# Layer C's prompt attention with key tiles of 128, 128 and 16, and a new order of the steps of layers C and D

## The chip, the core and the metric

The kernel runs on one core of a Trainium2 chip, as one launch. The metric is the device time of that launch in microseconds. A core has five engines that work side by side, each through its own instructions in order: TensorE (PE, matrix products; PEld is its loading of the stationary operand), VectorE (DVE), ScalarE (ACT), GpSimd (POOL) and SyncE (SP, which here only issues DMAs). Engines wait for each other by semaphores.

## The reference, cut to what matters

Four layers of different kinds act on 336 tokens: 64 of a running stream (the "sample") and 272 of a new one (16 meta tokens and 256 frames, the "prompt"). Layers A and B are two recurrences; the change leaves them alone. Layer C is attention over a compressed cache, layer D a convolution of 31 taps along time for each of 2048 channels.

```python
def mla_mixer(...):                                   # layer C, 16 heads
    q_lat, kv_lat, k_pe, g = split(u @ w_in)          # g: gate path
    s = (q_abs . keys_c + q_pe . keys_pe) * C_SCALE
    mask = k_chunk[None, :] <= q_chunk[:, None]       # chunks of 64 frames, meta tokens first
    p = softmax(where(mask, s, -inf))
    o = p @ values
    return (o * silu(g)) @ w_out

def conformer_mixer(...):                             # layer D
    a, b, g = split(u @ w_in)
    v = a * sigmoid(b)
    c = causal_dwconv(concat(buf, v), conv_w) + conv_b   # 31 taps
    c = silu(layernorm(c))
    return (c * silu(g)) @ w_out
```

A prompt frame sees the meta tokens, its own chunk of 64 and the chunks before. The 16 meta queries see only the 16 meta keys, so the queries of the prompt's rows 16 to 79 see 80 keys, the next 144, then 208, and the last 272. The sample's 64 queries see 528 cached keys and their own 64.

## The kernel before

Everything lies transposed: features on the 128 partitions, the 336 tokens along the free dimension. A weight tile is 128x1024 float32. It comes from memory on SP's queue (`wraw`, three buffers), ACT casts it to a rounded part (`whi`, line 323) and the difference (`wlo`, line 335) is taken on DVE, or on POOL for the tiles named in the list `PRM["lo"]`. PE then makes three products for each slice (`mm3`: high by high, high by low, low by high). The tile of weights for one gate or input column (`in_tile`) is 24 matmuls of 336 columns. `Weights.tick` and `step` run the casts some tiles ahead. In the other layers' products of plain float32 the trace shows two matmul passes for each call.

**Layer C** first makes its latent queries and keys (the head: `raw_tile` six times, `rope`, `kv`, `qn`, `tk`, where `tk` transposes the sample's new keys), and then works through eight pairs of heads. Each pair p has steps: `q0`, `q1` (queries, PE), `sqa`, `ssc`, `str`, `sol`, `sou` (sample: absorb, scores and softmax, transposes, latent output, output), and for each head t of the pair `psc`, `pso`, `ptr`, `pou` (prompt: scores, softmax, transposes, output); `k` and `v` make keys and values for two pairs at a time; `g` is a gate tile, 24 matmuls that depend on no step. `PRM["c"]` lists the steps with a lag each, and `c_steps` unrolls it; this is the order of the instructions on every engine. PSUM banks are few: `acc` has two, and `misc`, `sp`, `pt`, `o`, `ss` one each, so a step that writes `misc` waits until the reader of the step before is done. The prompt's scores of a head lie in one tile `P` of 128 rows by 432 columns, queries 16 to 143 with 144 keys, queries 144 to 271 with 272 keys, and the meta queries with 16. In `p_tr` PE transposes it in six pieces, three of 128 keys into `pt`, three of 16 meta keys into `misc` (one of them 16x16); ACT copies the first, DVE the second. `p_out` multiplies them by the values, with key tiles 0 to 15, 16 to 143 and 144 to 271: three products of 272, 256 and 128 columns, the first with only 16 rows.

**Layer D** makes input tiles b and a for each of 16 column tiles j, `dext` from them on DVE, stores it to memory and loads it back shifted (`store`, `shifts`, on SP's queue) so that `conv_pe` can do four taps in one group of four 32-column products. `npm[j]` is the number of such groups, `ngt[j]` the taps that ACT scales and POOL adds (`gq`, `gp`), and DVE does the rest (`conv_dve`, line 1621, a generator run by `pump`). `conv_pe(j)` comes two column tiles after j. Gate tiles lie between (`PRM["g"]`, `tg`). After column tile 15 the sums over all channels (`s`, made on POOL) go through PE for the mean and the variance; nothing of layer D's output can start ahead of that, but for gate tiles 14 and 15.

## Time and profile before

| | us |
|---|---|
| median of three runs (lowest and highest) | 1310.57 (1309.44 to 1312.44) |
| the profiled execution | 1316.76 |
| its span, from the first to the last instruction | 1315.0 |
| busy in it: PE, DVE, ACT, POOL | 1259.6, 893.1, 776.4, 290.4 |

All rows below come from that one profiled execution. Times in them count from its first instruction. Layer C runs from about 640 to 993, layer D from about 998 to the end. A matmul's end is modelled, and matmuls overlap; so what one costs in a stream is read from start to start and not from its duration.

### The profile page before, as it was taken

The numbers are of one execution on the slowest core, as the hardware profiler recorded it, in microseconds if no ns is written. First come the engines' busy times: TensorE is split into PE (matmuls) and PEld (weight loads), VectorE is DVE, ScalarE is ACT, GpSimd is POOL, SyncE is SP. The second block draws the span as 40 slices with busy tenths as digits, with TensorE's granted clock in tenths as the row PEclk, the third lists the DMA queues.
The fourth block names the chain that finished last, engine by engine and source line by source line (L and its number), as shares of the span: only waits on it lengthen the run. The fifth ranks groups of instructions, "written<-read, shape, count | busy, mean of one in ns | idle before, by whom it ended". The sixth has DMA issues, their size and how long they took to land.

```text
span 1315.0 us, 21810 instructions
## 1 busy us (share of the span) xinstructions
PE 1259.6 (96%) x8402; PEld 1185.7 (90%) x8402; DVE 893.1 (68%) x1654; ACT 776.4 (59%) x1448; POOL 290.4 (22%) x335
## 2 busy tenths in 40 slices
PE   8999999999999999899989999998999899999896
PEld 8999999999999999799879898887898789888795
DVE  5677666676658999957755555555657498886684
ACT  5677666667545877755554445444643756665563
POOL 0000000000001122100140000000002676878592
PEclk9999999999999999899989999899999899999999
DMA  6433343333441444344343222231242576767242
GB/s 211 142 124 92 125 126 107 131 126 104 137 145 66 145 145 145 113 147 144 110 158 105 88 89 81 67 99 60 91 150 71 165 199 179 208 178 196 77 139 74
DMA packets 58903, 166.25 MB, mean 126 GB/s; under 512 B 7616, under 2 KB 22048, under 8 KB 58800
## 3 DMA queue, kind: packets, MB, share of 16 engines
q1 hardware_dynamic: 55248, 157.28, 38.6%
q0 software_dynamic: 1504, 4.88, 1.2%
q10 hardware_dynamic: 2048, 2.70, 0.7%
q8 instruction: 66, 1.08, 0.3%
q14 instruction: 37, 0.30, 0.1%
HBM read 157.34 MB, written 7.50 MB: 125 GB/s over the span
## 4 chain that ended last, share of the span: by engine, by line
PE 71%; DVE 12%; ACT 6%; issue 3%; POOL 3%; DMA 2%; SPq 0%; ACTq 0%; DVEq 0%; POOLq 0%
PE acc L395 41%; PE bacc L395 9%; PE cv L395 3%; PE o L395 3%; PE hacc L395 3%; DVE wlo L335 2%; PE y L395 2%; PE sp L395 2%; ACT Pp L1450 2%; PE ss L395 2%; ACT whi L323 1%; PE misc L395 1%; DVE cv L1621 1%; POOL wlo L335 1%; DMA wraw<-in_wts_dram 1%
## 5 line engine op out<-in xcount | busy, mean ns | idle before, releaser
L395 PE MATMUL acc<-uh,whi 128*128 128x336 f32 x1208 | 390.5, 323 | 1.8 <-ACT vv L979 1.8
L395 PE MATMUL acc<-uh,wlo 128*128 128x336 f32 x1208 | 384.2, 318 | 0.0
L395 PE MATMUL acc<-ul,whi 128*128 128x336 f32 x1208 | 383.5, 317 | 0.0
L323 ACT ACTIVATE whi<-wraw 128x1024 fp32r<-128x1024 f32 (+2 forms) x263 | 269.0, 1028 | 91.2 <-DMA wraw<-in_wts_dram 64.0
L335 DVE TENSOR_TENSOR wlo<-wraw,whi 128x1024 fp32r<-128x1024 f32 (+2 forms) x233 | 286.1, 1243 | 25.2 <-ACT whi L323 24.7
L395 PEld LDWEIGHTS acc<-uh,whi 128*128 128x128 f32 x1208 | 228.8, 189 | 11.6 <-issue 5.0
L395 PEld LDWEIGHTS acc<-ul,whi 128*128 128x128 f32 x1208 | 228.9, 189 | 0.5 <-issue 0.2
L395 PEld LDWEIGHTS acc<-uh,wlo 128*128 128x128 f32 x1208 | 227.9, 189 | 0.0
L687 POOL TENSOR_TENSOR x<-x,sroot 128x336 f32<-128x336 f32 x6 | 5.3, 897 | 533.5 <-ACT sroot L675 390.6
L1621 DVE SCALAR_TENSOR_TENSOR cv<-dext,dw,cv 128x366 f32<-128x366 f32 x184 | 97.3, 594 | 3.5 <-PE cv L395 2.7
L1613 POOL TENSOR_TENSOR gp<-gp,gq 128x366 f32<-128x366 f32 x77 | 90.0, 1170 | 36.1 <-ACT gq L1612 32.2
L395 PE MATMUL bacc<-oh,whi 128*128 128x336 f32 x288 | 92.1, 320 | 0.0
L395 PE MATMUL bacc<-oh,wlo 128*128 128x336 f32 x288 | 91.3, 317 | 0.0
L395 PE MATMUL bacc<-ol,whi 128*128 128x336 f32 x288 | 91.1, 316 | 0.0
L335 POOL TENSOR_TENSOR wlo<-wraw,whi 128x1024 fp32r<-128x1024 f32 (+1 forms) x30 | 67.3, 2248 | 18.2 <-ACT whi L323 18.2
L395 PE MATMUL acc<-oh,whi 128*128 128x336 f32 x192 | 61.5, 320 | 1.9 <-ACT dsg L1665 1.1
L395 PE MATMUL acc<-ol,whi 128*128 128x336 f32 x192 | 61.1, 318 | 1.3 <-DVE ol L421 0.8
L395 PE MATMUL acc<-oh,wlo 128*128 128x336 f32 x192 | 60.9, 317 | 0.7 <-DVE wlo L335 0.7
L1450 ACT ACTIVATE Pp<-sp,mx 64x80 f32<-64x80 f32 (+4 forms) x80 | 30.0, 375 | 45.9 <-DVE mx L1448 26.0
L395 PEld LDWEIGHTS bacc<-ol,whi 128*128 128x128 f32 x288 | 54.2, 188 | 0.4
L395 PEld LDWEIGHTS bacc<-oh,whi 128*128 128x128 f32 x288 | 54.2, 188 | 0.4
L395 PEld LDWEIGHTS bacc<-oh,wlo 128*128 128x128 f32 x288 | 54.1, 188 | 0.0
(436 smaller groups left out, 2561.8 us busy)
## 6 DMA issues: line engine op xcount, KB each, us to landing
wraw<-in_wts_dram SPq DMA_DIRECT2D x243, 512.0 KB, 3.6
dsh<-dxt SPq DMA_DIRECT2D x60, 189.0 KB, 4.2
wraw<-in_wts_dram SPq DMA_DIRECT2D x16, 384.0 KB, 3.0
dxt<-dext SPq DMA_DIRECT2D x15, 198.0 KB, 4.1
out_hg_dram<-sf SPq DMA_DIRECT2D x16, 128.0 KB, 2.1
wraw<-in_wts_dram SPq DMA_DIRECT2D x8, 256.0 KB, 2.7
ukt<-in_ukt_dram POOLq DMA_DIRECT2D x8, 256.0 KB, 3.3
uv<-in_wts_dram POOLq DMA_DIRECT2D x8, 256.0 KB, 3.9
```

What stands on the lines that cost most here:

```text
L323: self.nc.scalar.activation(hi[:, :n], self.raw[i][:, :n], AF.Copy)
L335: e.tensor_tensor(lo[:, :n], self.raw.pop(i)[:, :n], hi[:, :n].bitcast(F32), op=OP.subtract)
L395: self.PE.matmul(out, l, r, start=start, stop=stop)
L687: G.tensor_tensor(self.x[:, k], self.x[:, k], sq, op=OP.mult)
L1450: A.activation(P[r0:r1, c:c + n], s[r0:r1, c:c + n], AF.Exp, scale=C_SCALE, bias=mx[r0:r1, j:j + 1], accum_out=sm[r0:r1, j:j + 1])
L1613: G.tensor_tensor(cv[j, "p"], cv[j, "p"], q, op=OP.add)
L1621: V.scalar_tensor_tensor(c[:, :T], ext[j % NX][:, n:n + T], tap(n, j), c[:, :T], op0=OP.mult, op1=OP.add)
```

## The change

Layer C: the values are made for key tiles 0 to 127, 128 to 255 and 256 to 271. `P` is 544 columns wide, holds the long part first, and is zero where nothing is written. `p_tr` makes one product with 16 columns of the identity and five transposes of 128x128, and reads over the zeros, so that all pieces have 128 rows and 128 columns; `pl` (128x64, zero but for 16 rows) holds the last 16 keys. `p_out` then has products of 272, 192 and 64 columns, each with 128 rows. The third product of `values` has a stationary operand of 16 columns. In the head, the cache comes in five DMAs, where it was eight; the constant `k_pair` is gone, and two products by columns take its place; the sample's new keys stand behind the cached ones; their evacuation is on DVE.

The tables: `c` has one gate tile behind `tk`, one less in pair 1, and in pair 2 one ahead of the softmax of head 1 where it was behind its transposes. In D `npm[9]` is 3 (was 4), `ngt` and `pump` change, and the gate tiles near the end stand later. 15 tiles' `wlo` go from DVE to POOL (ten of layer C, five of D), four of D go back.

```diff
--- before.py
+++ after.py
@@ -35,27 +35,28 @@
...
-    "npm": [0, 2, 4, 3, 3, 2, 4, 3, 4, 4, 4, 4, 4, 4, 4, 3],
+    "npm": [0, 2, 4, 3, 3, 2, 4, 3, 4, 3, 4, 4, 4, 4, 4, 3],
...
-    "ngt": [5, 5, 2, 6, 4, 7, 4, 3, 7, 7, 9, 7, 3, 9, 1, 14],
-    "act": [1, 9, 6, 79, 2],
...
-    "g": [0, 0, 0, 0, 1, 0, 1, 0, 2, 1, 1, 0, 1, 0, 1, 0],
...
+    "ngt": [3, 5, 2, 6, 6, 7, 4, 3, 7, 8, 8, 7, 2, 10, 1, 15],
+    "act": [0, 8, 7, 80, 2],
...
+    "g": [0, 0, 0, 0, 1, 0, 1, 0, 2, 1, 1, 0, 1, 0, 0, 0],
...
-    "tg": [3, 2],
...
+    "tg": [2, 2],
...
+          ["do1", 15], ["do1", 13], ["do1", 6], ["da", 2], ["do1", 5], ["do1", 3], ["do1", 11], ["cg", 6], ["cg",
+          2], ["da", 13], ["db", 15], ["cg", 4], ["co2", 11], ["dg", 7], ["cun", 2], ["da", 4], ["dg", 12], ["co2",
+          15], ["cg", 7], ["cup", 6], ["cup", 4], ["co2", 8], ["da", 10]],
...
-        "k_pair": np.ascontiguousarray(pm.reshape(128, -1)),
...
+            G.memset(keyk[:48, 4], 0.0)
...
-            loads = [(keyt[:, l, a:b], self.d["ct"][:, l, c:d])
-                     for l in range(2) for a, b, c, d in ((0, 512, 0, 512), (576, NK, 512, NCACHE))]
-            loads += [(kps[:, :512], self.d["cr"][:, :512]), (kps[:, 576:], self.d["cr"][:, 512:]),
-                      (keyk[:, :4], self.d["ck"]), (keyk[64:80, 4], self.d["ckt"])]
+
+            loads = [(keyt[:, l, :NCACHE], self.d["ct"][:, l]) for l in range(2)]
+            loads += [(kps[:, :NCACHE], self.d["cr"]), (keyk[:, :4], self.d["ck"]), (keyk[48:64, 4], self.d["ckt"])]
...
-            G.tensor_copy(keyt[:, :, 512:576], kr[:, :, :NS])
-            G.tensor_copy(kps[:, 512:576], kpe[:, :NS])
+            G.tensor_copy(keyt[:, :, NCACHE:], kr[:, :, :NS])
+            G.tensor_copy(kps[:, NCACHE:], kpe[:, :NS])
...
-            A.activation(keyk[:64, 4], tp[:64, :256], AF.Copy)
+            V.tensor_copy(keyk[64:, 4], tp[:64, :256])
...
+            pl = [tm.tile([128, 64], F32, name=f"ppl{t}") for t in range(2)]
             for t in range(2):
-                z = tm.tile([128, 432], F32, name=f"Pp{t}")
+                G.memset(pl[t], 0.0)
+                z = tm.tile([128, 544], F32, name=f"Pp{t}")
...
-                        V.tensor_tensor(qs, qp[:, :NS].unsqueeze(1).to_broadcast([128, 2, 64]), pm, op=OP.mult)
+                        for h in range(2):
+                            V.tensor_scalar(qs[:, h], qp[:, :NS], self.col(f"m{h}"), None, op0=OP.mult)
...
-                for j, (c, w) in enumerate(((0, 16), (16, 128), (144, 128))):
-                    a = self.acc()
-                    z = slice(c, c + 128)
+                G.memset(vt[:, 2], 0.0)
+                for j, (c, w) in enumerate(((0, 128), (128, 128), (256, 16))):
+                    a = self.acc()[:w]
+                    z = slice(c, c + w)
                     for k in range(2):
                         self.mm3(a, kvh[:, k, z], kvl[:, k, z], h[:, k], l[:, k], k == 0, k == 1)
-                    A.activation(vt[:w, j], a[:w], AF.Copy)
+                    A.activation(vt[:w, j], a, AF.Copy)
...
-                self.PE.transpose(b[:80, :128], P[:, 512:], self.ident)
+                self.PE.transpose(b[:, :128], P[:, NK - 128:], self.ident)
                 pt = tm.tile([128, 5, 128], F32, name="spt")
                 A.activation(pt[:, :4].rearrange("p a b -> p (a b)"), a, AF.Copy)
-                V.tensor_copy(pt[:80, 4], b[:80, :128])
+                V.tensor_copy(pt[:, 4], b[:, :128])
...
+                         (0, 16, 416, 16, 2, 416))
+                for r0, r1, c, n, j, _ in parts:
                     V.tensor_reduce(mx[r0:r1, j:j + 1], s[r0:r1, c:c + n], axis=AX, op=OP.max)
                 V.tensor_scalar(mx, mx, -C_SCALE, None, op0=OP.mult)
-                for r0, r1, c, n, j in parts:
-                    A.activation(P[r0:r1, c:c + n], s[r0:r1, c:c + n], AF.Exp, scale=C_SCALE, bias=mx[r0:r1, j:j + 1],
+                for r0, r1, c, n, j, o in parts:
+                    A.activation(P[r0:r1, o:o + n], s[r0:r1, c:c + n], AF.Exp, scale=C_SCALE, bias=mx[r0:r1, j:j + 1],
                                  accum_out=sm[r0:r1, j:j + 1])
                 rs = tm.tile([128, 3], F32, name="rs")
                 V.reciprocal(rs, sm)
-                V.tensor_scalar(P[:, :144], P[:, :144], rs[:, 0:1], None, op0=OP.mult)
-                V.tensor_scalar(P[:, 144:416], P[:, 144:416], rs[:, 1:2], None, op0=OP.mult)
-                V.tensor_scalar(P[:16, 416:], P[:16, 416:], rs[:16, 2:3], None, op0=OP.mult)
+                V.tensor_scalar(P[:, :272], P[:, :272], rs[:, 1:2], None, op0=OP.mult)
+                V.tensor_scalar(P[:, 272:416], P[:, 272:416], rs[:, 0:1], None, op0=OP.mult)
+                V.tensor_scalar(P[:16, 416:432], P[:16, 416:432], rs[:16, 2:3], None, op0=OP.mult)
...
             def p_tr(p, t):
                 P = Pp[t][0]
...
-                tr(a[:, 0:128], P[:, 16:144], self.ident)
-                tr(a[:, 128:256], P[:, 160:288], self.ident)
-                tr(a[:, 256:384], P[:, 288:416], self.ident)
-                tr(b[:16, 0:16], P[:16, 416:432], self.ident[:16, :16])
-                tr(b[:16, 16:144], P[:, 0:16], self.ident)
-                tr(b[:16, 144:272], P[:, 144:160], self.ident)
-                pt = tm.tile([128, 384], F32, name="ppt")
-                pm_ = tm.tile([16, NP], F32, name="ppm")
-                A.activation(pt, a[:, :384], AF.Copy)
-                V.tensor_copy(pm_, b[:16, :NP])
-                H[p, t] = (pt, pm_)
+                self.mm(a[:, 0:16], P[:, 416:544], self.ident[:, :16])
+                tr(a[:, 208:336], P[:, 400:528], self.ident)
+                tr(a[:, 16:144], P[:, 272:400], self.ident)
+                tr(a[:, 144:272], P[:, 0:128], self.ident)
+                tr(a[:, 336:464], P[:, 128:256], self.ident)
+                tr(b[:, :128], P[:, 256:384], self.ident)
+                pt = tm.tile([128, 464], F32, name="ppt")
+                A.activation(pt, a[:, :464], AF.Copy)
+                V.tensor_copy(pl[t][:16], b[:16, 64:128])
+                H[p, t] = pt
 
             def p_out(p, t):
-                pt, pm_ = H.pop((p, t))
+                pt = H.pop((p, t))
                 vt = quadw[p // 2][1]
                 z = slice(128 * (2 * (p % 2) + t), 128 * (2 * (p % 2) + t) + 128)
                 o = bank("o")
-                self.mm(o[:, :NP], vt[:16, 0, z], pm_, True, False)
-                self.mm(o[:, 16:NP], vt[:, 1, z], pt[:, :256], False, False)
-                self.mm(o[:, 144:NP], vt[:, 2, z], pt[:, 256:], False, True)
+                self.mm(o[:, :NP], vt[:, 0, z], pt[:, :272], True, False)
+                self.mm(o[:, 80:NP], vt[:, 1, z], pt[:, 272:], False, False)
+                self.mm(o[:, 208:NP], vt[:, 2, z], pl[t], False, True)
```

On PE, a prompt head's transposes and output, at pair 1 of layer C. `Pp` is the tile P, `pt` and `misc` are PSUM, `ppt` and `ppm` or `ppl` are the copies, `vt` the values. Before:

```order
L1462 MATMUL pt<-ident,Pp_7262 128x128
L1463 MATMUL pt<-ident,Pp_7262 128x128
L1464 MATMUL pt<-ident,Pp_7262 128x128
L1465 MATMUL misc<-ident,Pp_7262 16x16
L1466 MATMUL misc<-ident,Pp_7262 16x128
L1467 MATMUL misc<-ident,Pp_7262 16x128
L395 MATMUL o<-ppm,vt 128x272
L395 MATMUL o<-ppt,vt 128x256
L395 MATMUL o<-ppt,vt 128x128
```

And in the changed kernel:

```order
L395 MATMUL pt<-ident,Pp_7261 128x16
L1468 MATMUL pt<-ident,Pp_7261 128x128
L1469 MATMUL pt<-ident,Pp_7261 128x128
L1470 MATMUL pt<-ident,Pp_7261 128x128
L1471 MATMUL pt<-ident,Pp_7261 128x128
L1472 MATMUL misc<-ident,Pp_7261 128x128
L395 MATMUL o<-ppt,vt 128x272
L395 MATMUL o<-ppt,vt 128x192
L395 MATMUL o<-ppl_7259,vt 128x64
```

The pieces of 16 rows and 16 columns are gone, and the products are 272, 192 and 64 columns wide, each from 128 rows.

On DVE, at pair 2 of layer C, from the queries' mask (`qs`) on; `mx` is the softmax's maximum of head 1, `sg<-sq,acc` a gate tile's evacuation. Before:

```order
L1328 TENSOR_TENSOR qs<-qp,pm 128x128
L1447 TENSOR_REDUCE mx_7270<-sp 64x1 x4
L1447 TENSOR_REDUCE mx_7270<-sp 16x1
L1448 TENSOR_SCALAR mx_7270<-mx_7270 128x3
L1453 RECIPROCAL rs<-sm_7271 128x3
L1454 TENSOR_SCALAR Pp_7268<-Pp_7268,rs 128x144
L1455 TENSOR_SCALAR Pp_7268<-Pp_7268,rs 128x272
L1456 TENSOR_SCALAR Pp_7268<-Pp_7268,rs 16x16
L1471 COPY ppm<-misc 16x272
L335 TENSOR_TENSOR wlo<-wraw,whi 128x1024
L1203 SCALAR_TENSOR_TENSOR sg<-sq,acc 128x336
```

And in the changed kernel:

```order
L1329 TENSOR_SCALAR qs<-qp,vec 128x64 x2
L335 TENSOR_TENSOR wlo<-wraw,whi 128x1024
L1201 SCALAR_TENSOR_TENSOR sg<-sq,acc 128x336
L1450 TENSOR_REDUCE mx_7270<-sp 64x1 x4
L1450 TENSOR_REDUCE mx_7270<-sp 16x1
L1451 TENSOR_SCALAR mx_7270<-mx_7270 128x3
L1456 RECIPROCAL rs<-sm_7271 128x3
L1457 TENSOR_SCALAR Pp_7268<-Pp_7268,rs 128x272
L1458 TENSOR_SCALAR Pp_7268<-Pp_7268,rs 128x144
L1459 TENSOR_SCALAR Pp_7268<-Pp_7268,rs 16x16
L1475 COPY ppl_7258<-misc 16x64
```

The evacuation of a gate tile, and the split of a weight tile ahead of it, now stand ahead of the softmax of head 1, which they followed.

On ACT, near the end of layer D's convolution, from the last tap that ACT scales for column tile 15 (`gq`); `dsg` is a gate's SiLU, `call` a convolution's finished column tile. Before (the cast of 128x768 is the first of the output weights):

```order
L1612 ACTIVATE gq<-dext_10632,dw 128x366 x2
L323 ACTIVATE whi<-wraw 128x768
L1665 ACTIVATE dsg<-acc 128x336
L1633 ACTIVATE call<-cv,vec 128x64
L1634 ACTIVATE call<-cv,vec 128x272
L1636 ACTIVATE sq<-call 128x336
```

And in the changed kernel:

```order
L1616 ACTIVATE gq<-dext_10628,dw 128x366
L323 ACTIVATE whi<-wraw 128x1024
L1669 ACTIVATE dsg<-acc 128x336
L1637 ACTIVATE call<-cv,vec 128x64
L1638 ACTIVATE call<-cv,vec 128x272
L1640 ACTIVATE sq<-call 128x336
```

The finished tiles now follow the SiLU of gate tile 11, where they followed that of tile 12. On PE one gate tile (24 matmuls) stood between the last `conv_pe` and the mean; now three stand there (72).

## Rows read from the trace of the kernel before

**Rows 1.** Page, part 1: busy time, share of the span, instructions.

```profile
PE 1259.6 (96%) x8402; PEld 1185.7 (90%) x8402; DVE 893.1 (68%) x1654; ACT 776.4 (59%) x1448; POOL 290.4 (22%) x335
```

**Rows 2.** Stretches: time, busy time and instructions by engine, granted clock, DMA share, GB/s.

```profile
645.00:653.00 8.00, 7.88 (x49) 7.41 (x49) 4.67 (x6) 4.97 (x12) 1.10 (x2) 1.00 1.00 325
841.00:848.00 7.00, 6.65 (x32) 6.09 (x32) 1.60 (x5) 0.87 (x2) 1.69 (x4) 0.56 0.47 151
1180.00:1200.00 20.00, 20.00 (x161) 16.64 (x151) 8.44 (x18) 10.28 (x20) 18.56 (x14) 1.00 0.71 192
```

**Rows 3.** Timeline, PE, an output of pair 0: start, duration, engine, line, operation [idle before <-releaser].

```profile
710.23 1.00 PE L395 MATMUL misc<-olat,uv 128*128 128x64 f32 x8
711.15 0.72 PE L395 MATMUL o<-ppm,vt 16*128 16x272 f32 x2
...
712.56 1.05 PE L395 MATMUL misc<-qn,ukt 128*128 128x64 f32 x8
713.42 0.40 PE L395 MATMUL acc<-uh,whi 128*128 128x336 f32 x1
```

**Rows 4.** Timeline, PE, pair 0, transposes of head 1.

```profile
720.91 0.27 PE L1462 MATMUL pt<-ident,Pp 128*128 128x128 f32 x1
...
721.13 0.27 PE L1464 MATMUL pt<-ident,Pp 128*128 128x128 f32 x1
721.34 0.18 PE L1465 MATMUL misc<-ident,Pp 16*16 16x16 f32 x1
...
721.59 0.38 PE L395 MATMUL ss<-ksh,qabh 128*128 128x296 f32 x1
721.81 0.30 PE L395 MATMUL ss<-ksl,qabh 128*128 128x296 f32 x1
```

**Rows 5.** Timeline, PE, pair 4, scores of head 1 and the sample's output.

```profile
831.10 0.41 PE L395 MATMUL sp<-kp,qp 128*128 128x144 f32 x2
831.35 0.62 PE L395 MATMUL sp<-kn,qn 128*128 128x272 f32 x2
831.81 0.62 PE L395 MATMUL sp<-kp,qp 128*128 128x272 f32 x2
...
839.27 0.77 PE L395 MATMUL misc<-olat,uv 128*128 128x64 f32 x5 [0.89 <-DVE ppm L1471]
```

**Rows 6.** Timeline, DVE and ACT, pair 4, softmax of head 1.

```profile
833.68 1.56 DVE L1447 TENSOR_REDUCE mx<-sp 64x1 f32<-64x80 f32 x5
...
837.96 0.18 DVE L1453 RECIPROCAL rs<-sm 128x3 f32<-128x3 f32 x1 [2.51 <-ACT Pp L1450]
...
838.79 0.42 DVE L1471 COPY ppm<-misc 16x272 f32<-16x272 f32 x1
...
839.15 0.42 ACT L1202 ACTIVATE sq<-acc 128x336 f32<-128x336 f32 x1
```

**Rows 7.** Timeline, ACT and DVE, head of layer C.

```profile
653.48 1.06 ACT L323 ACTIVATE whi<-wraw 128x1024 fp32r<-128x1024 f32 x1 [3.51 <-DMA wraw<-in_wts_dram]
...
659.28 1.22 DVE L335 TENSOR_TENSOR wlo<-wraw,whi 128x1024 fp32r<-128x1024 f32 x1
```

**Rows 8.** Timeline, PE and SP's queue, layer D.

```profile
1078.10 2.05 PE L395 MATMUL cv<-dsh,dcw 128*32 128x366 f32 x24 [1.38 <-DMA dsh<-dxt]
...
1060.40 5.77 SPq L304 DMA_DIRECT2D wraw<-in_wts_dram  x2
```

**Rows 9.** Timeline, DVE and PE, end of layer D's convolution.

```profile
1219.72 4.65 DVE L1621 SCALAR_TENSOR_TENSOR cv<-dext,dw,cv 128x366 f32<-128x366 f32 x9 [2.75 <-PE cv L395]
...
1226.63 2.33 PE L395 MATMUL cv<-s,onesE 128*128 128x336 f32 x4 [3.08 <-POOL s L1640]
1228.76 1.33 PE L395 MATMUL cv<-call,onesE 128*128 128x336 f32 x2
```

**Rows 10.** Timeline, POOL and DVE, two splits at once.

```profile
1203.17 2.40 POOL L335 TENSOR_TENSOR wlo<-wraw,whi 128x1024 fp32r<-128x1024 f32 x1
...
1204.60 2.06 DVE L335 TENSOR_TENSOR wlo<-wraw,whi 128x1024 fp32r<-128x1024 f32 x1
```

More of the change, by code (lines that the diff above doesn't have):

```diff
@@ L44 @@
     "bt": [3, 1, 9, 13, 15, 24, 18, 9, 12, 6, 16, 17, 18, 24],
-    "npm": [0, 2, 4, 3, 3, 2, 4, 3, 4, 4, 4, 4, 4, 4, 4, 3],
+    "npm": [0, 2, 4, 3, 3, 2, 4, 3, 4, 3, 4, 4, 4, 4, 4, 3],
     "idle": [12, 8],
-    "ngt": [5, 5, 2, 6, 4, 7, 4, 3, 7, 7, 9, 7, 3, 9, 1, 14],
-    "act": [1, 9, 6, 79, 2],
-    "pump": [[9, 8, 3, 0, 4], [6, 4, 6, 0, 6]],
[9 rows of a table removed]
+    "ngt": [3, 5, 2, 6, 6, 7, 4, 3, 7, 8, 8, 7, 2, 10, 1, 15],
+    "act": [0, 8, 7, 80, 2],
+    "pump": [[8, 6, 2, 0, 4], [4, 4, 6, 0, 5]],
[10 rows of a table added]
 }
@@ L1178, in layer_c @@
             rp = cp.tile([128, 2, NT], F32, name="rp")
-            pm = cp.tile([128, 2, 64], F32, name="pm")
             ksh = cp.tile([128, 3, NK], F32R, name="ksh")
@@ L1183, in layer_c @@
             keyk = cp.tile([128, 5, 256], F32, name="keyk")
+            G.memset(keyk[:48, 4], 0.0)
             kps = wt.tile([128, NK], F32, name="kps")
             nc.gpsimd.dma_start(rp.rearrange("p a b -> p (a b)"), self.d["k_rope"])
-            nc.gpsimd.dma_start(pm.rearrange("p a b -> p (a b)"), self.d["k_pair"])
-            loads = [(keyt[:, l, a:b], self.d["ct"][:, l, c:d])
-                     for l in range(2) for a, b, c, d in ((0, 512, 0, 512), (576, NK, 512, NCACHE))]
-            loads += [(kps[:, :512], self.d["cr"][:, :512]), (kps[:, 576:], self.d["cr"][:, 512:]),
-                      (keyk[:, :4], self.d["ck"]), (keyk[64:80, 4], self.d["ckt"])]
+            loads = [(keyt[:, l, :NCACHE], self.d["ct"][:, l]) for l in range(2)]
+            loads += [(kps[:, :NCACHE], self.d["cr"]), (keyk[:, :4], self.d["ck"]), (keyk[48:64, 4], self.d["ckt"])]
             def rope(out, ps):
@@ L1412, in s_olat @@
                     for j in range(5):
-                        w = 128 if j < 4 else 80
-                        self.mm(a[:, 128 * l:128 * l + 128], keyk[:w, j, 128 * l:128 * l + 128], pt[:w, j], j == 0, j == 4)
+                        self.mm(a[:, 128 * l:128 * l + 128], keyk[:, j, 128 * l:128 * l + 128], pt[:, j], j == 0, j == 4)
                 o = tm.tile([128, 2, 128], F32, name="olat")
@@ L1444, in p_soft @@
                 P, mx, sm = Pp[t]
-                parts = ((0, 64, 0, 80, 0), (64, 128, 0, 144, 0), (0, 64, 144, 208, 1), (64, 128, 144, 272, 1), (0, 16, 416, 16, 2))
-                for r0, r1, c, n, j in parts:
+                parts = ((0, 64, 0, 80, 0, 272), (64, 128, 0, 144, 0, 272), (0, 64, 144, 208, 1, 0), (64, 128, 144, 272, 1, 0),
+                         (0, 16, 416, 16, 2, 416))
+                for r0, r1, c, n, j, _ in parts:
                     V.tensor_reduce(mx[r0:r1, j:j + 1], s[r0:r1, c:c + n], axis=AX, op=OP.max)
                 V.tensor_scalar(mx, mx, -C_SCALE, None, op0=OP.mult)
-                for r0, r1, c, n, j in parts:
-                    A.activation(P[r0:r1, c:c + n], s[r0:r1, c:c + n], AF.Exp, scale=C_SCALE, bias=mx[r0:r1, j:j + 1],
+                for r0, r1, c, n, j, o in parts:
+                    A.activation(P[r0:r1, o:o + n], s[r0:r1, c:c + n], AF.Exp, scale=C_SCALE, bias=mx[r0:r1, j:j + 1],
                                  accum_out=sm[r0:r1, j:j + 1])
```

18 rows, old and new, of the table PRM are left out of this document.

## The prediction

> **What bounds the kernel now.** I read part 1 of the page first: PE is busy 1259.6 of 1315.0 us [rows 1], so only work on PE, or a wait of PE, can move the end. I then went through PE's timeline of layers C and D, subtracting a stream's usual spacing, and looked at what released each idle stretch. The reader is to see three things. First, layer C holds pieces that cost more than their columns: between two runs of eight 64-column passes, three products take 712.56 - 710.23 = 2.33 us, eight passes included [rows 3]. Second, the waits are short and end in DVE's queue, as the 0.89 us ahead of the sample's output in pair 4 [rows 5]. Third, layer D loses most at one place, the barrier at its end, where PE stands idle 3.08 us and then works slowly [rows 9].
>
> **Layer C, outputs.** The same eight passes with nothing foreign behind them take 713.42 - 712.56 = 0.86 us, so the three products with their changes of shape cost 2.33 - 0.86 = 1.47 us [rows 3]. After, they are two passes of each width. A pair of 272 columns takes 831.81 - 831.35 = 0.46, one of 144 columns 831.35 - 831.10 = 0.25 [rows 5], so 192 columns take about 0.33 by the line between. A 64-column pass takes 0.86 / 8, so the third pair 0.22. Together 1.00. The saving is 0.47 for each of 16 heads, **-7.5 us**. About 0.11 of the 0.47 is columns (528 instead of 656, at 0.46 / 272 for a pair's column, less the floor that the 64-column pair pays); the other 0.36 is the change between operands of 16 and of 128 rows, which goes. This is the largest term, and what it rests on is that the changes cost and not something that follows them.
>
> **Layer C, transposes.** Before, six pieces take 721.59 - 720.91 = 0.68, and the next product starts its successor 0.22 after itself where others do after 0.13 to 0.14 [rows 4]: 0.77 in all. After, there are seven passes (the product with the identity is two); the one that follows a transpose of the same shape comes 0.11 later (two steps from 720.91 to 721.13) [rows 4], so 0.77. **Nothing**, from -2.5 if passes of 16 columns take half that to +1 us.
>
> **Layer C, values.** The third product now has a stationary operand of 16 columns. The step into such a form is 721.34 - 721.13 = 0.21 where 0.11 is usual, so 0.10; the way out I take as 0.18, the larger of the two sides of the output's changes. Four times 0.28: **+1.1 us**.
>
> **Layer C, waits.** In pairs 4 and 6 the sample's output waits 0.89 us for the copy of the transposes [rows 5], which on DVE stands behind head 1's softmax. That chain does not shorten, but PE comes 0.47 earlier by the cheaper output ahead of it. The copy is 0.2 shorter (64 columns), and the queries' mask is two instructions where it was one, about 0.1 longer. So PE waits 0.37 more at both: **+0.7**. In pair 2 a gate tile now precedes the softmax on DVE, as the order shows. From its last matmul on there are its SiLU on ACT, 0.42 [rows 6], its product on DVE, which I estimate at 0.48 from the copy's 0.42 for 272 columns, and then maximum to copy, 838.79 + 0.42 - 833.68 = 5.5 less 0.2 [rows 6]: 6.2 us. PE has the transposes, an output and one gate tile in that time, 0.77 + 1.00 + 24 x 0.16 = 5.6, the 0.16 being 7.88 us / 49 matmuls [rows 2]. That leaves 0.6, and the steps from engine to engine add to it: **+0.7**, between 0 and +1.5. These stay small because each is paid once.
>
> **Layer C, head.** One split of 1.22 us on DVE, between two steps of the chain that PE waits for [rows 7], goes to POOL: -1.2. Against it, the cached keys' transposed copy is now loaded sooner, into a stretch in which the DMA engines are full (share 1.00, 325 GB/s, 645 to 653) and ACT waits 3.51 us for a weight tile [rows 2, 7]. Its 524 KB at 325 GB/s are 1.6 us; if the half of it lands ahead of the weights, +0.8. One evacuation less on ACT, -0.2. **-0.6**, from -3.5 to +1.5. Sum of layer C: -7.5 + 1.1 + 0.7 + 0.7 - 0.6 = **-5.6 us**.
>
> **Layer D, one tap group less.** `npm[9]` loses four products of two passes. A tile with three groups has 24 passes in 2.05 us [rows 8]; eight passes fewer are 0.68 by that, less something for a fixed part: **-0.6**. The taps that it takes over are on DVE (+3 in all, 4.65 / 9 = 0.52 each [rows 9]); DVE works 8.44 of 20 us in the stretch before the end [rows 2], so they hide there. If that cover is gone, 1.5 us.
>
> **Layer D, a late transfer.** At 1078.10 PE waits 1.38 us for a shifted tile [rows 8]. SP's queue, which issues it, stood 5.77 us at a weight tile whose buffer a split on POOL still held [rows 8]. That split (`da` 5) goes back to DVE, where one takes 1.22 [rows 7]. But `da` 4 goes to POOL just ahead. **-0.9**, between -1.4 and +1.
>
> **Layer D, the end.** Before, one gate tile lies between the last `conv_pe` and the mean, and PE waits 3.08 us for POOL's sums; its first four passes of 336 columns then take 1228.76 - 1226.63 = 2.13 us [rows 9], where 0.46 / 2 for 272 columns [rows 5] makes 4 x 0.28 = 1.1. After, three gate tiles lie there, 2 x 24 x 0.16 = 7.7 us more cover, while conv 15 comes no later than DVE's 2.75 us wait for it allows [rows 9]. I take the wait, 1.3 for the slow passes (1.0 in these four, 0.3 in those behind) and 0.4 for small gaps, an estimate: **-4.8**, from 0 to -5.2. What is late next: ACT's taps, 15 of the last tile instead of 14, and POOL's sums behind them; they have 4 us of margin. Sum of layer D: -0.6 - 0.9 - 4.8 = **-6.3 us**.
>
> **The sum.** -11.9 us. The profiled execution would go from 1316.76 to 1304.9; it is 6.2 above the median of 1310.57, and what lies outside the span stays at 1.8. By the median: 1310.57 - 11.9 = **1298.7 us**. A measurement of this kernel can tell 0.2%, 2.6 us.
>
> **Rivals.** (A) The changes of rows cost nothing of their own, and what follows them absorbs it. Then layer C's outputs save the columns alone, 16 x 0.11 = 1.8, and 5.7 of the sum goes: 1304.4 us. Against it stands that the pair of 272 columns with 128 rows takes 0.46 [rows 5], while the whole group of 656 columns, some 1.1 by that rate, took 1.47 [rows 3]. The Trainium skill, "TensorE: Matmul & The Clock Gate", section "Why this matters for your kernels", says that a single product with 32 rows takes the time of one with 128; by that rule zeros instead of few rows bring nothing. The trace differs, at the changes at least, by the 0.36 us above. Chance 0.06.
>
> (B) The end does not move: with POOL given five more splits in D, at 18.56 busy of 20 us just before [rows 2], its sums come as late relative to the gate tiles as before. Then -4.8 goes: 1303.5. Against it stands the 7.7 us of cover. Chance 0.10.
>
> (C) Slower. Seven splits of layer C now on POOL run beside DVE's chain from softmax to copy. Two splits side by side took 2.40 on POOL and 2.06 on DVE [rows 10] where DVE alone needs 1.22 [rows 7]. If each stops a DVE instruction of that chain for its whole 2.4 us, and PE's waits there are already above zero [rows 5], 7 x 2.4 = 16.8 us come on top: 1315.5. It decides as soon as a split starts just ahead of a rotation or a difference with two operands in the chain, and the chain has no slack. Against it: 2.06 - 1.22 = 0.84 is what one overlap cost, and most splits have a gate tile's 24 x 0.16 = 3.8 us ahead of them. The Trainium skill, "SBUF — State Buffer", section "Who interferes with whom", says that a DVE instruction with two SBUF inputs contends with a GpSimd instruction that reads SBUF; the trace agrees, by these 0.84 us. Chance 0.08.
>
> (D) The new short waits bring a fall of the clock. From 841 to 848 the granted clock is 0.56 with PE busy 6.65 of 7 us [rows 2], behind the wait at 839.27 [rows 5]: 7 x 0.44 = 3.1 us. Three more of them: +9.2, 1307.9. Chance 0.06.
>
> **How the numbers follow.** The forecast has 0.70, the rest is shared as said: A .06, B .10, C .08, D .06. Range: the open ends are the head (-2.9, +2.1), the transposes (-2.5, +1), the late transfer (-0.5, +1.9) and the end (-0.4, +4.8). Not all fall together: 1291 below; above, 1308, which takes in A, B and D and leaves out C and the sum of several bad ends. Faster by more than 0.2% means below 1307.9: forecast, A, B and most of D, 0.86. Same: the rest of D and of the forecast's own tail, 0.06. Slower: C, 0.08.
>
> **What would show it.** In the changed profile: the three outputs from start to next product in 1.0 us; transposes and the next start in 0.77; PE's wait for sums at the end gone, with the granted clock near 1 there; the wait at the sample's output in pairs 4 and 6 up to 1.3 us and a new one in pair 2; nothing above 0.5 for the shifted tile of 1078. I am wrong if outputs still take 1.4 us, if PE waits for DVE between softmax and copy in most pairs, or if the clock is below 0.97 over the span.

## The result

The changed kernel took 1299.87 us (median of four runs, 1298.90 to 1303.01), the kernel before 1310.01 in the same session; the ratio is 0.9924, with a 95% interval of 0.9902 to 0.9946. Timed twice more beside the experiments, the ratio was 0.9888 (0.9866 to 0.9910) and 0.9897 (0.9873 to 0.9920). The kernel is faster by 0.8 to 1.1%, 10 to 15 us. The forecast was 1298.7, with a range of 1291 to 1308.

The page of the changed kernel, part 1, answers to [rows 1]:

```profile
PE 1245.6 (96%) x8410; PEld 1182.8 (91%) x8410; DVE 886.6 (68%) x1655; ACT 778.5 (60%) x1448; POOL 317.1 (24%) x353
```

PE has 14 us less of busy time, and POOL 27 us more. PE's timeline where an output of pair 0 stands between 64-column products answers to [rows 3]:

```profile
710.48 1.00 PE L395 MATMUL misc<-olat,uv 128*128 128x64 f32 x8
711.31 1.00 PE L395 MATMUL o<-ppt,vt 128*128 128x272 f32 x4
712.15 0.33 PE L395 MATMUL o<-ppl,vt 128*128 128x64 f32 x2
712.32 1.10 PE L395 MATMUL misc<-qn,ukt 128*128 128x64 f32 x8
713.24 0.40 PE L395 MATMUL acc<-uh,whi 128*128 128x336 f32 x1
```

From the eight passes to the next eight, 712.32 - 710.48 = 1.84 us, where it was 2.33. The line of `o<-ppm,vt` with its 16 rows is gone. The waits at the sample's outputs of pairs 2, 4 and 6 answer to the 0.89 us of [rows 5]:

```profile
773.45 0.32 PE L395 MATMUL misc<-olat,uv 128*128 128x64 f32 x1 [0.81 <-DVE ppl L1475]
...
833.30 1.10 PE L395 MATMUL misc<-olat,uv 128*128 128x64 f32 x8 [1.32 <-DVE ppl L1475]
...
890.18 0.32 PE L395 MATMUL misc<-olat,uv 128*128 128x64 f32 x1 [1.32 <-DVE ppl L1475]
```

The mean at the end of layer D's convolution, answering to [rows 9], starts without an idle time, and its four passes take 1213.83 - 1212.70 = 1.13 us where they took 2.13:

```profile
1212.70 1.29 PE L395 MATMUL cv<-s,onesE 128*128 128x336 f32 x4
1213.83 0.73 PE L395 MATMUL cv<-call,onesE 128*128 128x336 f32 x2
```

Granted clock in stretches (columns as in [rows 2]); the first is pair 4's end, which was at 0.56 before, the second pairs 6 and 7 of layer C, the third the mean:

```profile
834.00:842.00 8.00, 7.67 (x56) 7.23 (x56) 3.50 (x9) 1.38 (x3) 2.04 (x4) 1.00 0.37 131
900.00:920.00 20.00, 17.29 (x115) 15.81 (x114) 10.14 (x31) 8.94 (x29) 0.00 (x0) 0.91 0.14 44
1212.00:1216.00 4.00, 4.00 (x21) 3.26 (x20) 0.77 (x2) 0.99 (x3) 3.26 (x2) 1.00 0.32 75
```

Read from starts of the same instruction in all profiles (the kernel before was profiled a second time, the changed one twice more, below), the stages are:

| stage, from PE's timeline | before, two profiles | changed, three profiles |
|---|---|---|
| start to the first prompt score of layer C | 694.0, 691.7 | 694.4, 693.8, 696.2 |
| from there to the last sum over layer C's output | 298.1, 298.0 | 287.9, 286.5, 286.5 |
| from there to the mean of layer D | 234.5, 233.4 | 230.5, 230.1, 230.2 |
| from there to the last sum | 78.1, 78.3 | 74.8, 74.7, 74.8 |

One gate tile of 3.8 us moved from the second stage to the first. So, by the means, the first is about 1.9 us shorter than it would be, the second about 7.3, the last two together 7.1. The 1.9 is no more than what profiles of one kernel differ by in that stage (2.3 and 2.4 us). The profiles sit wider apart than the medians (16 us against 10 to 15), since both profiles of before are above their median.

### The profile page after: what moved, and what is told of

Its sections match the earlier page's. It is cut to its first block, busy times and chain, and to the rows that moved or that the text cites. A ratio compares the mean times of both kernels' runs of the same rounds, so it can differ in the third digit from the quotient of the medians.

```text
span 1297.9 us, 21859 instructions
## 1 busy us (share of the span) xinstructions
PE 1245.6 (96%) x8410; PEld 1182.8 (91%) x8410; DVE 886.6 (68%) x1655; ACT 778.5 (60%) x1448; POOL 317.1 (24%) x353
## 4 chain that ended last, share of the span: by engine, by line
PE 69%; DVE 15%; ACT 7%; issue 3%; POOL 2%; DMA 2%; ACTq 0%; DVEq 0%; POOLq 0%
PE acc L395 40%; PE bacc L395 9%; DVE wlo L335 3%; PE cv L395 3%; PE hacc L395 3%; PE o L395 3%; PE y L395 2%; PE sp L395 2%; DVE cv L1625 2%; ACT Pp L1453 2%; PE ss L395 2%; DMA wraw<-in_wts_dram 1%; ACT whi L323 1%; PE misc L395 1%; PE x L395 1%
## 5 line engine op out<-in xcount | busy, mean ns | idle before, releaser
L335 DVE TENSOR_TENSOR wlo<-wraw,whi 128x1024 fp32r<-128x1024 f32 (+2 forms) x222 | 274.2, 1248 | 25.5 <-ACT whi L323 24.7
L335 POOL TENSOR_TENSOR wlo<-wraw,whi 128x1024 fp32r<-128x1024 f32 (+2 forms) x41 | 96.1, 2348 | 129.8 <-ACT whi L323 82.8
L1617 POOL TENSOR_TENSOR gp<-gp,gq 128x366 f32<-128x366 f32 x78 | 86.3, 1109 | 26.4 <-ACT gq L1616 22.7
```

Of the source, the lines that this page charges most:

```text
L335: e.tensor_tensor(lo[:, :n], self.raw.pop(i)[:, :n], hi[:, :n].bitcast(F32), op=OP.subtract)
L1617: G.tensor_tensor(cv[j, "p"], cv[j, "p"], q, op=OP.add)
```

## Experiments

Each kernel was timed in the same session as the kernel before (ratio and 95% interval), and profiled once.

**Only the new key tiles.** The kernel before with the new `values`, `p_soft`, `p_tr` and `p_out`, and the mask by columns in place of `k_pair`; its core:

```diff
-                for j, (c, w) in enumerate(((0, 16), (16, 128), (144, 128))):
+                for j, (c, w) in enumerate(((0, 128), (128, 128), (256, 16))):
...
-                self.mm(o[:, :NP], vt[:16, 0, z], pm_, True, False)
-                self.mm(o[:, 16:NP], vt[:, 1, z], pt[:, :256], False, False)
-                self.mm(o[:, 144:NP], vt[:, 2, z], pt[:, 256:], False, True)
+                self.mm(o[:, :NP], vt[:, 0, z], pt[:, :272], True, False)
+                self.mm(o[:, 80:NP], vt[:, 1, z], pt[:, 272:], False, False)
+                self.mm(o[:, 208:NP], vt[:, 2, z], pl[t], False, True)
```

> The kernel before with only the new key tiles (values, softmax into P of 544 columns, p_tr, p_out), the constant k_pair gone to make room; order, splits and layer D as before. Theory (the change between operands of 16 and of 128 rows costs by itself): three outputs from 1.47 to 1.00 us in 16 heads, values +1.1, waits at the sample's output of pairs 4 and 6 up by 0.37 each: 1310.0 - 7.5 + 1.1 + 0.7 = about 1304.3. Rival A (only columns count): 1310.0 - 1.8 + 1.1 + 0.3 = about 1309.6, and three outputs at 1.3 to 1.4 us in the trace.

1307.62 us against 1311.77: 0.9965 (0.9950 to 0.9980), that is 2.6 to 6.6 us less. This holds the theory's 5.7 and not the rival's 0.4. In its trace most outputs take 1.01 or 0.93 us, where they took 1.41 or 1.33; the rival had 1.3 to 1.4. Pair 4's wait is 1.29 us, as forecast. Layer C's stage of the table takes 290.9 us here, 7.1 less than before; the slow stretch of pair 4, of which more below, is not in this profile.

**The disputed cost by itself.** The changed kernel, with 16 rows in the third product:

```diff
-                self.mm(o[:, 208:NP], vt[:, 2, z], pl[t], False, True)
+                self.mm(o[:, 208:NP], vt[:16, 2, z], pl[t][:16], False, True)
```

> The changed kernel with one difference: the third product of each prompt output takes 16 rows of the values and of the last piece where it takes 128 (the others are zero). Theory: a product with 16 rows between products with 128 rows costs 0.36 us by its changes, 16 x 0.36 = +5.8: 5 to 6 us above the changed kernel of the same call, and the three outputs go from 1.01 to about 1.37 us in the trace. Rival A: rows do not count, no difference, 1.0 us in the trace.

1305.43 us, where the changed kernel of the same session took 1298.15: 7 us more. The ratios to before are 0.9939 (0.9916 to 0.9962) and 0.9888 (0.9866 to 0.9910). PE's timeline at the same place as above:

```profile
711.33 1.00 PE L395 MATMUL o<-ppt,vt 128*128 128x272 f32 x4
712.26 0.43 PE L395 MATMUL o<-ppl,vt 16*128 16x64 f32 x2
712.62 1.10 PE L395 MATMUL misc<-qn,ukt 128*128 128x64 f32 x8
```

The same 64 columns with 16 rows start 712.26 - 711.33 = 0.93 after the pairs of 272 and 192 columns, where those with 128 rows started 0.84 after, and the next product follows after 0.36 instead of 0.17. So one step in and one out cost 0.28 us together; in 16 outputs 4.5. It is less than the 0.36 that I had. Row count by itself is what changed here, since columns and the rest of the kernel are the same: rival A is out. The 4.5 are not the 7 by time, though. In layer C the waits at the sample's outputs give some of them back (0.47, 0.97 and 0.97 us, where the changed kernel has 0.81, 1.32 and 1.32), and its stage takes 289.9 us, 2.0 to 3.4 more. Layer D, whose instructions are the same, is 2.4 to 2.8 longer in this profile, with the clock at 0.85 from 995 to 1030 where the changed kernel has 0.95:

```profile
995.00:1030.00 35.00, 29.88 (x142) 25.35 (x142) 17.70 (x32) 20.95 (x47) 15.21 (x20) 0.85 0.28 87
```

So the price of the rows is read from the steps, and not from the time.

**Only the new head of layer C.** Five loads, the cached keys' copy loaded early, its rest on DVE, mask by columns:

```diff
-            loads = [(keyt[:, l, a:b], self.d["ct"][:, l, c:d])
-                     for l in range(2) for a, b, c, d in ((0, 512, 0, 512), (576, NK, 512, NCACHE))]
+            loads = [(keyt[:, l, :NCACHE], self.d["ct"][:, l]) for l in range(2)]
...
```

> The kernel before with only the new head of layer C (five loads, keyk loaded early, sample's keys behind the cached ones, evacuation on DVE, mask by columns). Theory: the early load takes 0.8 us from the weights, fewer instructions on ACT give 0.2 to 0.4 back: 1310.4, that is no change that timing tells; in the trace ACT's wait for a weight tile near 653 grows from 3.5 to between 4.0 and 5.1. Rival: the loads were what bound the head, and fewer of them give 2 us or more: 1308 or less, with that wait shorter than 3.5.

1314.99 us against 1311.77: 1.0019 (1.0003 to 1.0036). So it is slightly slower, not the gain of the rival. ACT's wait for the weight tile was 2.93 us; in the second profile of before it was 3.01. The wait that I took as the sign does not show the cost, and it stays open which step pays it.

**Only the new order in layer C.**

```diff
-          1], ["ssc", 0], ["g", [7, -1]], ["q0", -1], ["str", 0], ["psc0", 0], ["pso0", 0], ["q1", -1], ["sol", 0],
-          ["psc1", 0], ["k", -1], ["pso1", 0], ["ptr0", 0], ["g", [2]], ["pou1", 1], ["g", [4]], ["g", [0]], ["g",
+          0], ["g", [7, -1]], ["q0", -1], ["str", 0], ["g", [-2]], ["psc0", 0], ["pso0", 0], ["q1", -1], ["sol", 0],
+          ["psc1", 0], ["g", [2]], ["k", -1], ["pso1", 0], ["ptr0", 0], ["pou1", 1], ["g", [4]], ["g", [6]], ["g",
...
```

> The kernel before with only the new table of layer C's steps. Theory: in pair 2 the gate tile ahead of the softmax on DVE makes a new wait of 0.2 to 0.8 us at the sample's output (here the old output still covers 0.47 more), the gate tile behind tk moves the head's wait without shortening it: 1310.0 + 0.5 = 1310.5. Rival: the gate tile behind tk covers the waits of the head (2.6 us at the transposes, 2.0 at q0), and 1.5 to 2 us go: 1308.3.

1312.20 us against 1311.77: 0.9997 (0.9983 to 1.0012), no change. In the trace pair 2 has the new wait (0.50 us), the transposes still wait 2.59, and the gate tile's own wait of 3.13 has taken the place of q0's 2.0.

**The kernel before again.**

> The kernel before, unchanged, for a second profile. Theory: the profiled execution shown of it (1316.8, 6.2 above its median) had more stretches at the low clock than its other executions; a second profile near 1310 has two of them less, at about 3.4 us each, and 841 to 848 is at full clock. Rival: the stretch at 841 to 848 belongs to the kernel (it follows the 0.89 us wait) and is there again, at 0.56; then the saving after is partly that.

1312.80 against 1311.77, 1.0008 (0.9996 to 1.0021). The stretch at pair 4's end is there again at the low clock, here from the second profile of the kernel before:

```profile
840.00:850.00 10.00, 9.65 (x50) 9.13 (x51) 2.92 (x8) 2.77 (x6) 0.55 (x1) 0.68 0.27 98
```

It is not there in the changed kernel; this is the same stretch of its second profile:

```profile
830.00:850.00 20.00, 18.29 (x130) 17.00 (x128) 10.10 (x26) 9.67 (x29) 2.04 (x4) 1.00 0.29 93
```

But it does not belong to every execution of this layer C. The kernel with only layer D's tables (below) has the same layer C and the same wait, and its clock is full there:

```profile
838.55 0.32 PE L395 MATMUL misc<-olat,uv 128*128 128x64 f32 x1 [0.89 <-DVE ppm L1471]
...
840.00:850.00 10.00, 9.34 (x67) 8.70 (x65) 4.82 (x12) 3.26 (x7) 1.98 (x4) 1.00 0.33 106
```

What it cost I take from the time between the sample's output of pair 4 and the first score of head 1 in pair 5, whose lines are, in this order, of the kernel before, of the one with layer D's tables and of the changed kernel:

```profile
859.60 0.21 PE L395 MATMUL sp<-kn,qn 128*16 128x16 f32 x2 [0.26 <-ACT Pp L1450]
...
856.35 0.21 PE L395 MATMUL sp<-kn,qn 128*16 128x16 f32 x2 [0.25 <-ACT Pp L1450]
...
850.68 0.21 PE L395 MATMUL sp<-kn,qn 128*16 128x16 f32 x2 [0.25 <-ACT Pp L1453]
```

859.60 - 839.27 = 20.3 us with the slow stretch, 856.35 - 838.55 = 17.8 without it, and 850.68 - 833.30 = 17.4 in the changed kernel. So it costs 2.5 us where it comes. It came in four of the five profiles that have both the old order of layer C and the old key tiles, in one of them for half as long, and in none of the three of the changed kernel; how much of the gain by time is its going, these profiles do not tell.

**The changed kernel again.**

> The changed kernel, unchanged, timed again beside the others and profiled a second time. Theory: 10 to 12 us under the kernel before (ratio 0.991 to 0.9925), with the same waits in layer C (0.81 in pair 2, 1.32 in pairs 4 and 6) and one stretch at the low clock near 905. Rival: those waits or that stretch are of one execution, and differ here.

1298.15 against 1313.97, a ratio of 0.9888, more than was expected. The waits of layer C repeat (0.83, 1.29, 1.30), the stretch near 905 does not: its clock is 1.00 in this profile, 0.91 in the first.

**Only layer D's tables.**

```diff
-    "npm": [0, 2, 4, 3, 3, 2, 4, 3, 4, 4, 4, 4, 4, 4, 4, 3],
+    "npm": [0, 2, 4, 3, 3, 2, 4, 3, 4, 3, 4, 4, 4, 4, 4, 3],
...
-    "tg": [3, 2],
+    "tg": [2, 2],
...
```

> The kernel before with only layer D's tables new (npm, ngt, act, pump, g, t, tg), with the splits and layer C as before. Theory: -0.6 for the group of taps and -4.8 at the end, 5.4 us under the kernel before; in the trace PE does not wait for the sums ahead of the mean, and the clock is full there. Rival B: DVE, ACT or POOL end last there whatever PE does, and at most 0.6 us go.

1305.95 us against 1313.97: 0.9942 (0.9921 to 0.9963), 5 to 10 us less. PE's timeline at the mean, with no idle time ahead:

```profile
1218.13 1.29 PE L395 MATMUL cv<-s,onesE 128*128 128x336 f32 x4
1219.26 0.73 PE L395 MATMUL cv<-call,onesE 128*128 128x336 f32 x2
```

Rival B of this run is out. So is rival B of the prediction: the changed kernel, which has the five more splits on POOL, starts its mean without idle time as well. PE, not the sums, now sets the end of the convolution. From layer C's last sum to layer D's it takes 305.0 us here, as in the changed kernel (304.8 to 305.2), where it took 312.6 and 311.6: the whole gain of layer D is that of these tables. Which of them does how much was not tried.

**Only the splits on POOL.**

```diff
-    "lo": [["da", 5], ["da", 7], ["db", 2], ["db", 5], ["dg", 1], ["dg", 3], ["dg", 4], ["dg", 5], ["dg", 9], ["dg",
+    "lo": [["da", 7], ["db", 2], ["db", 5], ["dg", 1], ["dg", 3], ["dg", 4], ["dg", 5], ["dg", 10], ["do1", 4],
...
```

> The kernel before with only the new list of splits on POOL. Theory: the head of layer C gains the 1.2 us of a split on DVE or a little more (the 2.6 us wait at the transposes falls), the late transfer in layer D 0 to 1.4: 1 to 3 us under the kernel before. Rival C (a split on POOL stops DVE's instructions in the chain from softmax to copy for up to 2.4 us each, seven times): 5 to 17 us above it, with waits above 2 us at the sample's outputs of several pairs.

1315.29 us against 1312.56: 1.0014 (0.9994 to 1.0034). Neither the gain of the theory nor the loss of rival C. The waits at the sample's outputs are those of before (0.86 and 0.89 us). But SP's queue stands as long as before, and at 1076.83 PE waits longer than before, for DVE's taps:

```profile
1076.83 3.75 PE L396 MATMUL cv<-dsh,dcw 128*32 128x366 f32 x24 [3.76 <-DVE cv L1622]
```

That queue row (5.77 us at two weight tiles from 1059.02 on) is the one that I had put down to the split of `da` 5, which is back on DVE here. Counted along the list, the split on POOL that ends the wait is the sixth of layer D in the kernel before (1063.22, 2.57 us) and the sixth here (1061.84, 2.57 us), and the sixth is gate tile 1 in both lists: it never moved. With layer D's new tables the wait of 3.76 us is not there. The head's term was not tried by this run: the list names gate tile 2, which stands in the head in the new order only, so the head's splits stay on DVE here and the wait at the transposes is 2.60 us as before. So the list of splits does not pay by itself, and with the old taps it may cost; by time the interval holds no change.

**The copy ahead of the softmax.** The changed kernel, with head 0's transposes and the output of the pair before right behind the scores of head 1, so that DVE copies first:

```diff
-          ["psc1", 0], ["g", [2]], ["k", -1], ["pso1", 0], ["ptr0", 0], ["pou1", 1], ["g", [4]], ["g", [6]], ["g",
+          ["psc1", 0], ["pou1", 1], ["ptr0", 0], ["k", -1], ["pso1", 0], ["g", [2]], ["g", [4]], ["g", [6]], ["g",
```

> The changed kernel with another order of steps in layer C: the output of the pair before and the transposes of head 0 stand right behind the scores of head 1, so that on DVE the copy that the sample's output waits for stands ahead of the softmax of head 1; pair 2's gate tile is back behind that. Theory: the waits of 0.81, 1.32 and 1.32 us at the sample's output go, nothing else is late, since head 1's softmax is needed only in the next pair: 3.4 us under the changed kernel of the same call. Rival: the softmax comes 1 to 2 us later and something behind it (casts on ACT, transposes of head 1) is late by as much, in seven pairs: no gain, or up to 5 us slower.

1302.63 us, where the changed kernel took 1298.15; the intervals of their ratios to before overlap (0.9892 to 0.9938, and 0.9866 to 0.9910). The waits at the sample's outputs are gone, and others stand in their place, on PE and, behind that, DVE:

```profile
836.31 1.10 PE L392 MATMUL misc<-qn,ukt 128*128 128x64 f32 x8 [1.60 <-DVE sg L1426]
...
829.88 1.00 DVE L1447 TENSOR_REDUCE mx<-sp 64x1 f32<-64x208 f32 x3
833.56 0.18 DVE L1453 RECIPROCAL rs<-sm 128x3 f32<-128x3 f32 x1 [2.47 <-ACT Pp L1450]
...
835.98 0.27 DVE L1426 SCALAR_TENSOR_TENSOR sg<-misc,sg 128x128 f32<-128x128 f32 x1
```

The absorbed queries (`qn,ukt`) use the same bank as the sample's output, whose reader (`sg<-misc,sg`) now is the instruction behind the softmax: it waits 1.60 us here and 1.78 in pair 6. The clock also falls there, which it does not in the changed kernel (1.00 above):

```profile
830.00:850.00 20.00, 18.21 (x118) 17.24 (x117) 10.33 (x27) 7.71 (x20) 2.79 (x4) 0.91 0.27 78
```

A fall of the clock behind a new wait is what rival D of the prediction had; it stands here behind both waits (0.83 from 890 to 900, around the one of pair 6), in one profile. The rival of this run held in that nothing was gained: the waits moved, to a step that it had not named, and are as long in sum (1.60 + 1.78 us, against 0.81 + 1.32 + 1.32).

**Gate tiles as cover.** The changed kernel, with the early gate tiles of pairs 1 and 3 as second ones ahead of the sample's outputs of pairs 4 and 6, and pair 2's behind the transposes:

```diff
-    "c": [["g", [2]], ["sou", 1], ["pou0", 1], ["sqa", 0], ["v", 0], ["g", [1]], ["g", [3]], ["ptr1", 1], ["ssc",
+    "c": [["g", [2]], ["sou", 1], ["pou0", 1], ["sqa", 0], ["v", 0], ["ptr1", 1], ["ssc",
...
-          ["psc1", 0], ["g", [2]], ["k", -1], ["pso1", 0], ["ptr0", 0], ["pou1", 1], ["g", [4]], ["g", [6]], ["g",
+          ["psc1", 0], ["k", -1], ["pso1", 0], ["ptr0", 0], ["g", [2]], ["pou1", 1], ["g", [4]], ["g", [4]], ["g", [6]], ["g", [6]], ["g",
```

> The changed kernel with three gate tiles of layer C elsewhere: those ahead of head 1's transposes in pairs 1 and 3 now stand as second tiles ahead of the sample's outputs of pairs 4 and 6, and pair 2's is back behind the transposes. Theory: the waits of 0.81, 1.3 and 1.3 us go since the chain from softmax to copy has 3.7 us more cover, and two waits of 0.34 us for the split of the absorbed queries come in pairs 1 and 3: 2.7 us under the changed kernel of the same call. Rival (as with the copy ahead of the softmax): the waits turn up at another step, or the clock falls behind a new wait, and nothing is gained.

1296.70 us, where the changed kernel of the same session took 1299.84; the ratios to before are 0.9878 (0.9853 to 0.9904) and 0.9897 (0.9873 to 0.9920). The 3.1 us are near the 2.7 expected, but the intervals overlap, so the time does not settle it. The trace does for the waits: the sample's output of pair 4 starts with no idle time, and the new waits are those of 0.3 to 0.4 us for the split of the absorbed queries, one in each of pairs 1 and 3:

```profile
830.08 0.44 PE L392 MATMUL misc<-olat,uv 128*128 128x64 f32 x3
...
774.82 0.33 PE L1469 MATMUL misc<-ident,Pp 128*128 128x128 f32 x1 [0.34 <-DVE qabl L1368]
```

**The same with the late load.** `keyk` and its rest are loaded behind the head's weights:

```diff
-                if loads:
+                if len(loads) > 2:
                     nc.scalar.dma_start(*loads.pop(0))
```

> The kernel of the moved gate tiles, with the cached keys' transposed copy (keyk and its 16-row rest) loaded behind the head's weights as in the kernel before. Theory: the early load takes DMA time from the weights, and without it the wait ahead of the sum of ksq (2.3 and 2.0 us in two profiles of the changed kernel) falls to 0.6 to 1.6, as in the kernels with the late load: 1 us under the kernel of the moved gate tiles. Rival: the wait has another cause (the evacuation on DVE, or another split of the work): no difference.

1296.90 against 1296.70: no difference. The wait ahead of the sum of `ksq` fell from 2.63 to 1.38 us, and a wait of 0.95 at the transposes came. In the six profiles that have the early load and gate tile 2's split on POOL that first wait is 1.8 to 2.7 us, so the early load may take something there; but one of the six has the wait at the transposes too (0.94 us, in the kernel with 16 rows), and the time does not change.

**The changed kernel a third time.**

> The changed kernel, unchanged, as the measure for the two kernels with moved gate tiles. 10 to 15 us under the kernel before, with waits of 0.8, 1.3 and 1.3 us at the sample's outputs.

1299.84 against 1312.56, with waits of 0.81, 1.29 and 1.32 us.

## Why the prediction was right, and where it was not

**Outputs and transposes.** Most outputs take 0.40 us less from their first product to what follows, in all three profiles (16.1 us in 16 heads where it was 21.9; in pairs 4 and 6 the product behind one of them comes later, and it saves less), and eight of them another 0.09 on the way in (0.83 from 710.48 to 711.31, against 0.92 in [rows 3]). That is 5.8 + 0.7 = 6.5 us, where the forecast had 7.5: its 0.47 holds for the eight heads whose output stands between 64-column products, and the others save 0.40. The mechanism is that of the last-16-rows kernel, 0.28 for the rows; with the forecast's 0.11 for the columns it makes about the 0.40. The transposes take 0.72 where they took 0.85 when an output follows, and 0.64 for 0.67 otherwise, 1.0 to 1.3 us in all, where the forecast had nothing. That the two together come to the 7.5 is luck.

**Values.** Here the step failed. A stationary operand of 16 columns costs nothing by its change. PE's timeline of `values` ahead of pair 4 in the kernel before, its first product and the next step's first:

```profile
812.53 0.47 PE L395 MATMUL acc<-whi,kvh 128*128 128x512 f32 x1
...
816.78 0.27 PE L1462 MATMUL pt<-ident,Pp 128*128 128x128 f32 x1
```

The same two in the changed kernel:

```profile
806.67 0.48 PE L395 MATMUL acc<-whi,kvh 128*128 128x512 f32 x1
...
810.94 0.29 PE L395 MATMUL pt<-ident,Pp 128*128 128x16 f32 x2
```

That is 4.25 and 4.27 us, +0.1 in four times where I had +1.1. I had taken the price from the step to the piece of 16x16 in [rows 4], which changes its rows and its columns at once; a change of columns alone costs 0.02 here.

**Waits of layer C.** 1.32 instead of 0.89 twice (+0.43 each, forecast +0.37), and 0.81 in pair 2 (forecast 0.7). Right.

**Head.** The size was near, the way was not. PE's three waits before ksq's sum, the transposes and q0 were 1.58 + 2.62 + 2.02 = 6.2 us (5.7 in the second profile); now there are two, 2.26 and 3.11, 5.4 in all (5.1 and, with a third one, 5.8 in the other profiles). The gain is no larger than that scatter. Taking the split off DVE freed the transposes altogether, and this took the new order and the new list together, since the split is that of gate tile 2, which the order brought into the head. But on POOL it ran beside the sum of squares. The timelines of POOL, DVE and PE in the changed kernel:

```profile
651.89 2.34 POOL L335 TENSOR_TENSOR wlo<-wraw,whi 128x1024 fp32r<-128x1024 f32 x1 [7.87 <-ACT whi L323]
...
652.51 2.09 DVE L1218 TENSOR_TENSOR ksq<-ksq,sq 128x336 f32<-128x336 f32 x1 [3.47 <-ACT sq L1216]
...
654.75 0.80 PE L395 MATMUL misc<-ksq,ones 128*128 128x336 f32 x2 [2.26 <-DVE ksq L1218]
```

And DVE's in the kernel with only the new order, where that split is on DVE:

```profile
652.06 0.51 DVE L1220 TENSOR_TENSOR ksq<-ksq,sq 128x336 f32<-128x336 f32 x1 [2.53 <-ACT sq L1218]
```

The instruction `ksq` with its two SBUF operands takes 2.09 us instead of 0.51. It did so in all seven profiles with that split on POOL at that place (2.08 to 2.12), and in none of the seven without (0.51). This is rival C's mechanism, at one place that PE waits for and for 1.6 us; the Trainium skill, "SBUF — State Buffer", section "Who interferes with whom", has the rule, and this trace agrees by those 1.6 us. The same stands at two more places in layer C, in all three profiles of the changed kernel, where PE had a gate tile to do: the last sum of a rotation takes 1.27 and 1.04 us instead of 0.51 beside a split on POOL. The first of them, on DVE:

```profile
703.07 1.27 DVE L1195 TENSOR_TENSOR qp<-qp,u 128x336 f32<-128x336 f32 x1
```

Between softmax and copy it did not happen. A list without the split of gate tile 2 was not tried.

**One tap group less.** Right: from the taps of column tile 9 to those of the next, PE takes 9.58 us where it took 10.22.

**The late transfer.** Wrong. The wait of 1.38 us in [rows 8] is gone, as forecast (those taps start at 1065.39 without idle time), but the taps of the next two column tiles now wait, the first 0.87 us for its shifted tile, the second 1.01 for DVE; in the second profile of before the wait was 0.51 to begin with:

```profile
1079.64 1.44 PE L395 MATMUL cv<-dsh,dcw 128*32 128x366 f32 x16 [0.87 <-DMA dsh<-dxt]
...
1089.71 1.13 PE L395 MATMUL cv<-dsh,dcw 128*32 128x366 f32 x12 [1.01 <-DVE cv L1625]
```

From the start of the taps ahead of the old wait to the start of those behind the second new one it takes 33.6 to 33.9 us, where it took 33.3 and 32.4. And the split of `da` 5 was not what held SP's queue: it was that of gate tile 1, as the splits-only kernel shows. I had matched the row to a name by the list and miscounted. Layer D's tables freed the queue: with them alone, and `da` 5 still on POOL, the two weight tiles take 1.95 us, and the wait is gone:

```profile
1055.75 1.95 SPq L304 DMA_DIRECT2D wraw<-in_wts_dram  x2
```

The -0.9 was read from one execution and one releaser.

**The end of layer D.** Right in kind. Wait and slow passes went, and both last stages together are 7.1 us shorter. Layer D's tables alone give 5 to 10. The 6.3 of my sum held the transfer's 0.9, which did not come; the end gave more than its 4.8. The last stage, from the mean on, is 3.4 us shorter, which is more than the 1.3 that I had for slow passes. 1.9 of it is gone by the first matmul behind the mean (2.01 us after the mean's start, 3.88 before); a wait for the last sums is 0.98 us, where it was 1.73, but 0.01 in the second profile of the changed kernel. I did not separate the rest.

**Not foreseen.** The slow stretch of pair 4, 2.5 us where it comes, was in both profiles of before and in none of the changed kernel. I had it in [rows 2] as the price of a rival, and did not ask whether the change would remove it. In the table it is part of layer C's 7.3 us. Since it is missing from one profile of the same layer C too, what its going gave by time is not known.

So the sum of -11.9 stands beside -10 to -15 by time. The two large terms, the cheaper outputs and the end of layer D, were right in kind: 6.5 us where I had 7.5, and some 6.5 (the 7.1 less the tap group) or more where I had 4.8. That the sum is so near is luck besides, since errors cancel: +1.0 for the values against -0.9 for the transfer, and the outputs' 1.0 too much against the transposes' 1.0 that I had at nothing. The slow stretch was not in it at all.
